# Dealing the first mixer's modulation columns out among the weight units of its second lane

## The chip, the core and the metric

The kernel runs on one core of a Trainium2 chip. The names in the profile are PE (TensorE's matrix multiplications) and PEld (its weight loads), DVE (VectorE), ACT (ScalarE), POOL (GpSimd) and SP (SyncE, which here issues every transfer between the chip's main memory and the core). Each engine works through its own list of instructions in a fixed order; semaphores make one engine wait for another. The metric is the device time of one execution in microseconds (us): the median of the runs, lower is better.

## The reference, cut to what matters

Two layers are computed on a sequence of 1024 positions of width 1024. Each layer is a mixing part and a feed-forward part, and both are steered by six modulation vectors that come from one vector `c`:

```
cond = silu(c)
mod = cond @ w_mod[l] + b_mod[l]
sh1, sc1, gt1, sh2, sc2, gt2 = split(mod, 6)
h = rms_norm(x, norm_g[l, 0]) * (1 + sc1) + sh1
y = mixer_block(h, ...)          # conv, sparse attention, linear attention, gMLP; then @ w_o
x = x + gt1 * rms_norm(y, norm_g[l, 1])
h = rms_norm(x, norm_g[l, 2]) * (1 + sc2) + sh2
y = square(relu(h @ w_up[l])) @ w_down[l]
x = x + gt2 * rms_norm(y, norm_g[l, 3])
```

What matters here are three of the six vectors of layer 0: number 2 (`gt1`), number 3 (`sh2`) and number 4 (`sc2`). They are needed only after the first mixer's output projection `w_o`.

## The kernel before, in words

The sequence is cut into two halves of 512 positions, so that every activation tile is 128 x 512. The order of the work is: first half's mixer of layer 0, `mix(0, 0)`; second half's mixer, `mix(0, 1)`; then feed-forward parts and the mixers of layer 1 in turn. The change lies in `mix(0, 0)` alone.

A projection (`gemm`, L177) takes its weights as two units of 128 x 512. A unit is loaded into a buffer `raw_b` (L158), copied to a rounded high part by ACT (L167), and DVE computes the low part (`sub`, recorded as L131); then twelve matrix multiplications follow, three for each of four slices (L173 to L175). There are two lanes of such weights in `mix(0, 0)`. Lane "a" feeds the sparse attention and `w_o`. Lane "b", with three `raw_b` buffers and four `w_b` buffers, feeds the projections of the linear attention (6), of the gMLP (4) and of the convolution (6): 16 projections, so 32 units. They are independent of the attention, and their multiplications fill PE between the attention's steps.

A modulation vector is eight columns of 128 values. A column (`mod_half`, L242) is two loads of 128 x 512 weights, each reduced on DVE against `cond` (L247) into one number per partition, and one small DVE instruction (L140, `mod<-mp,bmod`) that adds the two numbers and the bias. `mods_now(0, (2, 3, 4), "b")` computes 24 columns behind the convolution with lane "b"'s three `raw_b` buffers: 48 loads and 48 reductions.

After that come, in the program's order: the norm of the attention's output, splitting all eight mixer outputs into high and low parts (`split`, L220), the eight projections by `w_o` in lane "a" (16 units, 192 multiplications, each result copied by ACT at L946 into `yo`), then `between()`, which is the norm and modulation of the second half's input (`rms_R`, L186, and `make_h`, L203), and the residual, which uses vectors 2, 3 and 4.

What stands in which order on an engine is set when the program is built: a scheduler takes instructions whose inputs it believes to be ready by its own model, with earlier code first, and writes one fixed list for each engine. A buffer of a pool goes to the next user when the list says that it is free. All loads stand in one list, that of SP.

Of the kernel before, what the change touches and what calls it, by code (L numbers as in the profile page):

```python
# [35 lines left out]
def trunk_kernel(ctx, tc, xT, c, pos, freq, sel, w_in, conv_w, cmp_pos, cmp_w1, cmp_w2,  # L36
# [10 lines left out]
    def region(name, side="left"):  # L47
        return tc.tile_pool(name=name, bufs=1, reuse_waits="tile", side=side)
# [7 lines left out]
    def ps(tag, shape=(128, 512)):  # L56
        return psum.tile(list(shape), F32, name="ps_" + tag, tag=tag,
                         bufs={"mm": 2, "ff": 2, "s": 2, "t": 1, "pv": 1}[tag])
# [71 lines left out]
    def sub(out, a, b):  # L130
        V.tensor_tensor(out=out, in0=a, in1=b, op=ALU.subtract)  # L131

    def mul(out, a, b, eng=V):
        eng.tensor_tensor(out=out, in0=a, in1=b, op=ALU.mult)
# [4 lines left out]
    def stt(out, a, s, b, op0, op1):  # L139
        V.scalar_tensor_tensor(out=out, in0=a, scalar=s, in1=b, op0=op0, op1=op1)  # L140

    def load(tile, src):
        dma(out=tile, in_=src)
        return tile
# [11 lines left out]
    def wraw(lane, src, shape):  # L156
        raw = lane_pool[lane].tile(shape, F32, name="raw_" + lane, tag="raw_" + lane, bufs=RAWB[lane])
        dma(out=raw, in_=src)  # L158
        return raw

    def wtile(lane, shape):
        return lane_pool[lane].tile(shape, F32R, name="w_" + lane, tag="w_" + lane, bufs=HLB[lane])

    def wunit(lane, src, shape):
        raw = wraw(lane, src, shape)
        hi = wtile(lane, shape)
        A.copy(hi, raw)  # L167
        lo = wtile(lane, shape)
        sub(lo, raw, hi.bitcast(F32))
        return hi, lo  # L170

    def mm3(ps_ap, wh, wl, xh, xl, start, stop):
        PE.matmul(ps_ap, wh, xh, start=start, stop=False)  # L173
        PE.matmul(ps_ap, wh, xl, start=False, stop=False)  # L174
        PE.matmul(ps_ap, wl, xh, start=False, stop=stop)  # L175

    def gemm(ps_ap, lane, src, h, order=(0, 1, 2, 3, 4, 5, 6, 7)):  # L177
        for kh in (order[0] // 4, order[4] // 4):
            hi, lo = wunit(lane, src[:, 4 * kh:4 * kh + 4, :], [128, 4, 128])
            for kk in order:  # L180
                if kk // 4 == kh:
                    k = kk % 4
                    mm3(ps_ap, hi[:, k, :], lo[:, k, :], h[kk][0], h[kk][1],
                        kk == order[0], kk == order[7])

    def rms_R(tiles, inv_n, pt="t", cs=slice(0, T), mk=nt):  # L186
        acc = mk()[:, cs]
        A.activation(acc, tiles[0][:, cs], AF.Square)
        for t in tiles[1:]:
            sq = mk()[:, cs]  # L190
            A.activation(sq, t[:, cs], AF.Square)
            add(acc, acc, sq)
        p = ps(pt)[:, cs]
        with tc.high_priority(offset=400):
            PE.matmul(p, ones, acc, start=True, stop=True)  # L195
            return rstd(p, inv_n, mk()[:, cs])
# [17 lines left out]
    def group_out(y, pt, gain):  # L214
        R = rms_R(y, 1.0 / 256, pt)
        for k in range(2):
            stt(y[k], y[k], gain[:, k:k + 1], R, ALU.mult, ALU.mult)
        return y

    def split(t):  # L220
        hi, lo = htile(), htile()
        A.copy(hi, t)
        sub(lo, t, hi.bitcast(F32))
        return hi, lo
# [17 lines left out]
    def mod_half(l, j, k, mk):  # L242

        mp = work.tile([128, 2], F32, name="mp", tag="mp", bufs=4)
        for kh in range(2):
            raw = mk(w_mod[l, 8 * j + k, :, kh * T:kh * T + T], [128, T])
            V.tensor_tensor_reduce(out=raw, in0=raw, in1=cond[:, kh * T:kh * T + T], scale=1.0, scalar=0.0,  # L247
                                   op0=ALU.mult, op1=ALU.add, accum_out=mp[:, kh:kh + 1])
        stt(par[l]["mod"][:, j, k:k + 1], mp[:, 0:1], mp[:, 1:2], par[l]["bmod"][:, 8 * j + k:8 * j + k + 1],
            ALU.add, ALU.add)  # L250

    def mod_scale(l, j, ks):
        d = par[l]
        m = d["mod"][:, j, ks]
        if j in (1, 4):
            stt(d["A1" if j == 1 else "A2"][:, ks], m, 1.0, d["ng"][:, 0 if j == 1 else 2, ks],
                ALU.add, ALU.mult)
        if j in (2, 5):
            mul(d["G1" if j == 2 else "G2"][:, ks], m, d["ng"][:, 1 if j == 2 else 3, ks])
# [56 lines left out]
        return hs, early  # L316

    def mods_now(l, js, lane):
        for j in js:
            for k in range(8):  # L320
                mod_half(l, j, k, lambda src, shape: wraw(lane, src, shape))
            mod_scale(l, j, slice(0, 8))

    def mods_steps(todo, skip):

# [139 lines left out]
    def gate_part(l, hf, h, gr, rg, lane, early={}):  # L465
        p = early.get(GLA0)
        if p is None:
            p = ps("mm")
            gemm(p, lane, w_in[l, GLA0], h)
        lrT = rg.tile([32, T], F32, name="lrT")  # L470
        V.memset(lrT, 1.0)
        A.copy(lrT[0:16], p[0:16])
        gates = gr.tile([128, 4, 12], F32, name="gates")
        gtmp = gr.tile([128, 4, 12], F32, name="gtmp")
        gs = nt()
        A.copy(gs[0:64], p[0:64])
        gp = ps("t", (128, 4, 64))
        for j in range(4):
            PE.transpose(gp[:, j, :], gs[0:64, 128 * j:128 * j + 128], ident[0:64, 0:64])
        logsig(gates, gp[:, :, 32:44], gtmp)  # L480
        A.activation(gates, gates, AF.Exp)
        return gates, lrT
# [428 lines left out]
    def mix(l, hf, h, between=None, early={}):  # L911
        d = par[l]
        gain = d["gain"]
        with ExitStack() as es:
            gr = es.enter_context(region("gates"))
            if l == 0 and hf == 0:
                sx = ("ff", "ff", "ff")
                with region("wb", "right") as lane_pool["b"]:
                    with region("gl", "right") as rg:
                        gates, lrT = gate_part(l, hf, h, gr, rg, "a", early)  # L920
                        yn = nsa_part(l, hf, h, es.enter_context(region("ns")), gates, early)
                        ol = gla_part(l, hf, h, rg, "b", sx, lrT)
                    with region("cv", "right") as rg, region("gm", "right") as rg2:
                        og = gmlp_part(l, hf, h, rg2, "b", sx)
                        oc = conv_part(l, hf, h, rg, "b", sx)
                    mods_now(0, (2, 3, 4), "b")
            else:
                sx = ("s", "t", "pv")
                with region("cv") as rg, region("gm") as rg2:
                    oc = conv_part(l, hf, h, rg, "a", sx)  # L930
                    og = gmlp_part(l, hf, h, rg2, "a", sx)
                with region("gl") as rg:
                    gates, lrT = gate_part(l, hf, h, gr, rg, "a")
                    ol = gla_part(l, hf, h, rg, "a", sx, lrT)
                yn = nsa_part(l, hf, h, es.enter_context(region("ns")), gates)
            on = group_out(yn, "t", gain[:, 2:4])
            outs = [split(t) for t in oc + og + ol + on]
        res = None
        opening = (l, hf) == (0, 0)
        with region("wo", "right" if opening else "left") as rg:  # L940
            y = []
            for o in range(8):
                p = ps("mm")
                gemm(p, "a", w_o[l, o], outs, (6, 7, 4, 5, 2, 3, 0, 1) if opening else range(8))
                yo = rg.tile([128, T], F32, name="yo", tag="yo", bufs=8)
                A.copy(yo, p)  # L946
                y.append(yo)
            if between is not None:
                res = between()
            with tc.high_priority(offset=-LATER[l, hf]):  # L950
                R = rms_R(y, 1.0 / 1024)
                residual(y, d["G1"], R,
                         lambda k: load(rg.tile([128, T], F32, name="xo", tag="xo", bufs=8 if opening else 4),
                                        (xT[hf] if l == 0 else xb[hf])[:, k, :]), xa[l][hf])
                R = rms_R(y, 1.0 / 1024)
                h2[hf] = make_h(y, R, d["A2"], d["mod"][:, 3, :])
        if opening:
            lane_pool["f"] = pool("ff", side="right")
        return res
# [196 lines left out]
```

## Time and profile before

| What | Value |
|---|---|
| Median of 3 runs | 2634.32 us (2633.39 to 2635.1) |
| The profiled execution's own time | 2634.88 us |
| Its span, first to last instruction | 2633.1 us |
| PE busy over the span | 2488.4 us (95%) |
| DVE busy | 1631.0 us (62%) |
| ACT busy | 1310.5 us (50%) |
| Mean granted clock of TensorE | 0.975 of full speed |

The share of busy time is a mean over stages with different limits; the change is judged from its own stage, the first 360 us. Of the page's 40 slices of 65.8 us the fifth (263 to 329 us) shows PE at 4 tenths and a granted clock of 6 tenths, between slices at 9 and 9. A multiplication's duration in the trace is longer than the distance to the next one, since they overlap; pace is read from the distance between starts.

### The profile page before, as it was taken

How to read it: one execution, taken by the hardware profiler on the slowest of the kernel's cores; microseconds unless marked ns; L12 is line 12 of the kernel's file. 1: busy time of each engine (PE TensorE's matmuls, PEld its weight loads, DVE VectorE, ACT ScalarE, POOL GpSimd, SP SyncE). 2: the span in 40 equal slices, each digit the busy share in tenths (PEclk: the TensorE clock that was granted, in tenths of full speed). 3: DMA queues.
4: the chain of work that ended last, by engine and by line, in shares of the span. 5: the costliest groups of instructions: out<-in, count | busy, mean ns of one | idle time of the engine just before them, and what ended most of it. 6: DMA issues, size and time to landing. Idle time of an engine off the chain costs nothing.

```text
span 2633.1 us, 34406 instructions
## 1 busy us (share of the span) xinstructions
PE 2488.4 (95%) x11834; PEld 1987.3 (75%) x11834; DVE 1631.0 (62%) x3425; ACT 1310.5 (50%) x2657; POOL 53.0 (2%) x65
## 2 busy tenths in 40 slices
PE   5899499999999999999999999999999998899997
PEld 3666277777877878887787878877788876788886
DVE  7676866557888577444676476544567755634445
ACT  3573345445665356344366445444466744443333
POOL 0100000000000000000100000000100000000000
PEclk9899699999999999999999999999999999999999
DMA  8313634345434454322522344322322134433332
GB/s 279 100 46 100 203 117 132 106 140 153 129 123 134 155 164 140 102 85 89 154 83 70 116 152 140 99 84 79 119 77 68 57 108 143 136 97 96 97 97 75
DMA packets 176200, 305.79 MB, mean 116 GB/s; under 512 B 21573, under 2 KB 33434, under 8 KB 176026
## 3 DMA queue, kind: packets, MB, share of 16 engines
q1 hardware_dynamic: 176026, 303.60, 36.7%
q8 instruction: 93, 1.52, 0.2%
q14 instruction: 81, 0.66, 0.1%
HBM read 281.50 MB, written 17.83 MB: 114 GB/s over the span
## 4 chain that ended last, share of the span: by engine, by line
PE 83%; DVE 6%; DMA 4%; issue 1%; ACT 1%; POOL 0%; DVEq 0%; SPq 0%; ACTq 0%; POOLq 0%
PE ps_ff L173 16%; PE ps_ff L174 16%; PE ps_ff L175 16%; PE ps_mm L173 8%; PE ps_mm L175 8%; PE ps_mm L174 8%; DMA raw_f<-in_w_mod_dram 2%; PE ps_pv L783 1%; PE ps_mm L777 1%; PE ps_pv L782 1%; PE ps_s L822 1%; DMA raw_b<-in_w_mod_dram 1%; PE ps_s L824 1%; PE ps_t L777 1%; PE ps_t L195 1%
## 5 line engine op out<-in xcount | busy, mean ns | idle before, releaser
L167 ACT CAST w_f<-raw_f 128x512 fp32r<-128x512 f32 x504 | 311.7, 619 | 426.3 <-PE ps_ff L174 409.2
L131 DVE TENSOR_TENSOR w_f<-raw_f,w_f 128x512 fp32r<-128x512 f32 x504 | 350.4, 696 | 178.7 <-ACT w_f L167 167.9
L173 PE MATMUL ps_ff<-hid,w_f 128*128 128x512 f32 x992 | 395.4, 399 | 21.7 <-DVE yf L137 12.7
L175 PE MATMUL ps_ff<-h,w_f 128*128 128x512 f32 x1024 | 405.4, 396 | 1.2 <-DVE w_f L131 1.2
L173 PE MATMUL ps_ff<-h,w_f 128*128 128x512 f32 x1024 | 403.1, 394 | 0.0
L174 PE MATMUL ps_ff<-h,w_f 128*128 128x512 f32 x1024 | 402.3, 393 | 0.0
L174 PE MATMUL ps_ff<-hid,w_f 128*128 128x512 f32 x992 | 392.4, 396 | 1.5 <-DVE hid L131 1.5
L175 PE MATMUL ps_ff<-hid,w_f 128*128 128x512 f32 x992 | 391.7, 395 | 0.0
L173 PE MATMUL ps_mm<-h,w_a 128*128 128x512 f32 x784 | 318.2, 406 | 32.6 <-ACT yo L946 23.7
L175 PE MATMUL ps_mm<-h,w_a 128*128 128x512 f32 x784 | 317.2, 405 | 6.0 <-DVE w_a L131 6.0
L174 PE MATMUL ps_mm<-h,w_a 128*128 128x512 f32 x784 | 314.8, 403 | 3.6 <-DVE h L131 3.6
L167 ACT CAST w_a<-raw_a 128x512 fp32r<-128x512 f32 x196 | 121.3, 620 | 304.5 <-PE ps_mm L174 278.7
L131 DVE TENSOR_TENSOR w_a<-raw_a,w_a 128x512 fp32r<-128x512 f32 x196 | 135.1, 689 | 179.2 <-ACT w_a L167 173.3
L173 PEld LDWEIGHTS ps_ff<-hid,w_f 128*128 128x128 f32 x992 | 188.1, 190 | 69.8 <-DVE yf L137 15.2
L175 PEld LDWEIGHTS ps_ff<-h,w_f 128*128 128x128 f32 x1024 | 192.3, 188 | 45.5 <-issue 2.9
L173 PEld LDWEIGHTS ps_ff<-h,w_f 128*128 128x128 f32 x1024 | 192.4, 188 | 43.0 <-issue 3.1
L174 PEld LDWEIGHTS ps_ff<-h,w_f 128*128 128x128 f32 x1024 | 192.4, 188 | 42.0 <-issue 2.2
L174 PEld LDWEIGHTS ps_ff<-hid,w_f 128*128 128x128 f32 x992 | 188.3, 190 | 44.6 <-issue 2.9
L175 PEld LDWEIGHTS ps_ff<-hid,w_f 128*128 128x128 f32 x992 | 187.9, 189 | 41.1 <-issue 1.4
L137 DVE TENSOR_TENSOR y<-y,ps_ff 128x512 f32<-128x512 f32 (+1 forms) x208 | 138.0, 664 | 125.0 <-PE ps_ff L175 123.8
L173 PEld LDWEIGHTS ps_mm<-h,w_a 128*128 128x128 f32 x784 | 149.9, 191 | 72.8 <-ACT yo L946 24.1
L175 PEld LDWEIGHTS ps_mm<-h,w_a 128*128 128x128 f32 x784 | 149.8, 191 | 44.5 <-DVE w_a L131 7.7
(390 smaller groups left out, 3610.2 us busy)
## 6 DMA issues: line engine op xcount, KB each, us to landing
raw_f<-in_w_up_dram SPq DMA_DIRECT2D x256, 256.0 KB, 2.7
raw_f<-in_w_down_dram SPq DMA_DIRECT2D x256, 256.0 KB, 2.7
raw_a<-in_w_in_dram SPq DMA_DIRECT2D x132, 256.0 KB, 2.6
raw_f<-in_w_mod_dram SPq DMA_DIRECT2D x112, 256.0 KB, 2.9
raw_a<-in_w_o_dram SPq DMA_DIRECT2D x64, 256.0 KB, 2.7
raw_b<-in_w_mod_dram SPq DMA_DIRECT2D x48, 256.0 KB, 3.1
mw<-in_w_mod_dram SPq DMA_DIRECT2D x16, 512.0 KB, 5.7
bp<-in_cmp_w_dram SPq DMA_DIRECT2D x32, 256.0 KB, 5.7
```

The costliest lines, as they stand in the source:

```text
L131: V.tensor_tensor(out=out, in0=a, in1=b, op=ALU.subtract)
L137: eng.tensor_tensor(out=out, in0=a, in1=b, op=ALU.add)
L167: A.copy(hi, raw)
L173: PE.matmul(ps_ap, wh, xh, start=start, stop=False)
L174: PE.matmul(ps_ap, wh, xl, start=False, stop=False)
L175: PE.matmul(ps_ap, wl, xh, start=False, stop=stop)
L195: PE.matmul(p, ones, acc, start=True, stop=True)
L777: PE.transpose(tp[0:kn, hh, :], cols(h0 + hh), ident)
L782: PE.matmul(pv[:, h0:h0 + nh, :], vst, th[0:kn], start=first[0], stop=False)
L783: PE.matmul(pv[:, h0:h0 + nh, :], vst, tl[0:kn], start=False, stop=last)
L822: PE.matmul(sp[:, 0:w], qh[:, h0 + hh, :], KX[:, 128 * k0:128 * k0 + w], start=True, stop=False)
L824: PE.matmul(sp[:, 0:w], ql[:, h0 + hh, :], KX[:, 128 * k0:128 * k0 + w], start=False, stop=True)
```

## The change

`mods_now` becomes a generator that stops after each column. At every unit of lane "b", after the unit is loaded and split and before its multiplications, `gemm` asks the generator for one column. Vector order becomes 2, 4, 3. Whatever is left after the convolution is then computed as before; with 32 units and 24 columns nothing is left.

```diff
+    beside = {}
+
     def gemm(ps_ap, lane, src, h, order=(0, 1, 2, 3, 4, 5, 6, 7)):
         for kh in (order[0] // 4, order[4] // 4):
             hi, lo = wunit(lane, src[:, 4 * kh:4 * kh + 4, :], [128, 4, 128])
+            if lane in beside:
+                next(beside[lane], None)
...
     def mods_now(l, js, lane):
         for j in js:
             for k in range(8):
                 mod_half(l, j, k, lambda src, shape: wraw(lane, src, shape))
-            mod_scale(l, j, slice(0, 8))
+                if k == 7:
+                    mod_scale(l, j, slice(0, 8))
+                yield
...
                 with region("wb", "right") as lane_pool["b"]:
+                    beside["b"] = mods_now(0, (2, 4, 3), "b")
...
-                    mods_now(0, (2, 3, 4), "b")
+                    for _ in beside.pop("b"):
+                        pass
```

Because the scheduler sets the lists, the diff does not tell where the instructions stand. Line numbers of the changed kernel are a few higher: L251 is what L247 was, L671 what L664 was, L213 what L209 was, L955 what L946 was.

SP's list at the start of lane "b" before (`in_w_in` are a unit's weights, `in_w_mod` those of a column, `p` and `qh`, `ql` belong to the attention):

```order
L158 DMA raw_b<-in_w_in_dram 128x512 x5
L725 DMA p<-in_cmp_pos_dram 64x32
L726 DMA p<-in_cmp_pos_dram 64x31
L725 DMA p<-in_cmp_pos_dram 64x32
L726 DMA p<-in_cmp_pos_dram 64x31
L767 DMA qh<-qh 64x2x128
L767 DMA ql<-ql 64x2x128
```

and of the change (with the numbers that tell tiles of one name apart):

```order
L158 DMA raw_b_1552<-in_w_in_dram 128x512
L158 DMA raw_b_1559<-in_w_mod_dram 128x512
L158 DMA raw_b_1562<-in_w_mod_dram 128x512
L158 DMA raw_b_1578<-in_w_in_dram 128x512
L158 DMA raw_b_1585<-in_w_mod_dram 128x512
L158 DMA raw_b_1588<-in_w_mod_dram 128x512
L158 DMA raw_b_1607<-in_w_in_dram 128x512
L158 DMA raw_b_1614<-in_w_mod_dram 128x512
L158 DMA raw_b_1617<-in_w_mod_dram 128x512
L732 DMA p_786<-in_cmp_pos_dram 64x32
L733 DMA p_786<-in_cmp_pos_dram 64x31
```

Ahead of the attention's first four loads stood five loads in three buffers; now there are nine in the same three buffers. The pattern of one unit and two column loads goes on for 24 units.

DVE's list at the same place before (`gates`, `qr`, `qh`, `ql`, `VS`, `VW` belong to the attention):

```order
L131 TENSOR_TENSOR KW<-p,KW 64x512
L131 TENSOR_TENSOR w_b<-raw_b,w_b 128x512 x2
L140 SCALAR_TENSOR_TENSOR gates<-ps_t,gtmp 128x48
L137 TENSOR_TENSOR qr<-p 128x512
L140 SCALAR_TENSOR_TENSOR g<-ps_ff,g 128x512
L664 STREAM_SHUFFLE p<-qs 128x512
L131 TENSOR_TENSOR VS<-ps_t,VS 128x4x64
```

and of the change, with numbers:

```order
L131 TENSOR_TENSOR w_b_1556<-raw_b_1552,w_b_1554 128x512
L251 ISA raw_b_1559,mp_1558<-raw_b_1559,cond_130 128x512
L251 ISA mp_1558 128x1
L251 ISA raw_b_1562,mp_1558<-raw_b_1562,cond_130 128x512
...
L140 SCALAR_TENSOR_TENSOR gates_662<-ps_t_666,gtmp_663 128x48
L137 TENSOR_TENSOR qr_717<-p_719,p_720 128x512
L140 SCALAR_TENSOR_TENSOR g_1534<-ps_ff_1529,g_1535 128x512
L140 SCALAR_TENSOR_TENSOR mod0_100<-mp_1558,bmod0_97 128x1
L671 STREAM_SHUFFLE p_726<-qs_716 128x512
L131 TENSOR_TENSOR w_b_1582<-raw_b_1578,w_b_1580 128x512
L251 ISA raw_b_1585,mp_1584<-raw_b_1585,cond_130 128x512
```

A column's two reductions now stand among the attention's own DVE work, and each reads a load that was queued behind an earlier buffer's release.

ACT's list at the output projection before (`h<-nt` is `make_h` of the second half, `yo` the copy that frees a result buffer of PE; the last of the eight `h` rows and the two behind it):

```order
L199 ACTIVATE nt_3083<-ps_t_3081,eps_78 128x512
L200 ACTIVATE nt_3083<-nt_3083 128x512
L167 CAST w_a_2845<-raw_a_2843 128x512
L209 ACTIVATE h_3088<-nt_3086,mod0_100 128x512
...
L209 ACTIVATE h_3130<-nt_3128,mod0_100 128x512
L946 COPY yo_2783<-ps_mm_2746 128x512
L946 COPY yo_2822<-ps_mm_2785 128x512
```

and of the change:

```order
L955 COPY yo_2783<-ps_mm_2746 128x512
L203 ACTIVATE nt_3083<-ps_t_3081,eps_78 128x512
L204 ACTIVATE nt_3083<-nt_3083 128x512
L213 ACTIVATE h_3088<-nt_3086,mod0_100 128x512
L167 CAST w_a_2827<-raw_a_2825 128x512
L213 ACTIVATE h_3094<-nt_3092,mod0_100 128x512
L167 CAST w_a_2845<-raw_a_2843 128x512
L213 ACTIVATE h_3100<-nt_3098,mod0_100 128x512
L955 COPY yo_2822<-ps_mm_2785 128x512
```

All eight `h` activations stood ahead of the first two copies of results; now the first copy stands ahead of all of them and the second behind three. DVE's list there has the same work without the 48 reductions, and SP's list goes straight on with the loads of `w_o`. From `mix(0, 1)` on the lists of both kernels soon are the same.

## Rows read from the trace of the kernel before

**Rows 1.** Busy time by stage: length, PE, PEld, DVE, ACT, POOL, clock, DMA

```profile
core 0: us, PE busy (x) PEld busy (x) DVE busy (x) ACT busy (x) POOL busy (x), PEclk, DMA share, GB/s
75.00:103.00 28.00, 17.50 (x192) 15.31 (x192) 19.70 (x59) 13.59 (x47) 7.26 (x6) 0.68 0.29 78
103.00:145.00 42.00, 42.00 (x219) 34.08 (x222) 27.74 (x87) 29.52 (x80) 0.00 (x0) 0.97 0.25 69
145.00:180.00 35.00, 34.99 (x226) 26.08 (x218) 29.40 (x94) 26.90 (x71) 2.90 (x5) 1.00 0.14 46
...
200.00:236.00 36.00, 35.02 (x180) 27.01 (x180) 23.03 (x37) 17.08 (x32) 0.00 (x0) 0.98 0.20 65
236.00:256.20 20.20, 20.14 (x89) 16.34 (x87) 12.34 (x28) 4.86 (x8) 0.00 (x0) 1.00 0.41 132
256.20:319.30 63.10, 19.59 (x55) 12.29 (x55) 56.77 (x152) 23.17 (x39) 0.64 (x1) 0.63 0.64 202
```

**Rows 2.** PE's timeline, 255 to 356: start, duration, idle before

```profile
255.76 0.39 PE L175 MATMUL ps_mm<-h,w_b 128*128 128x512 f32 x1
261.00 2.07 PE L195 MATMUL ps_ff<-nt,ones 128*128 128x512 f32 x2 [4.85 <-DVE nt L137]
...
276.54 0.79 PE L173 MATMUL ps_mm<-h,w_a 128*128 128x512 f32 x1 [7.02 <-ACT h L222]
280.92 0.80 PE L174 MATMUL ps_mm<-h,w_a 128*128 128x512 f32 x1 [3.58 <-DVE h L131]
...
295.20 0.40 PE L175 MATMUL ps_mm<-h,w_a 128*128 128x512 f32 x1
319.29 0.80 PE L173 MATMUL ps_mm<-h,w_a 128*128 128x512 f32 x1 [23.70 <-ACT yo L946]
...
324.42 0.39 PE L173 MATMUL ps_mm<-h,w_a 128*128 128x512 f32 x1
...
354.99 0.40 PE L175 MATMUL ps_mm<-h,w_a 128*128 128x512 f32 x1
```

**Rows 3.** ACT's timeline, 256 to 322: start, duration, idle before

```profile
258.40 0.63 ACT L191 ACTIVATE nt<-of 128x512 f32<-128x512 f32 x1 [7.26 <-DVE of L134]
...
318.04 0.72 ACT L209 ACTIVATE h<-nt,mod 128x512 fp32r<-128x512 f32 x1 [0.68 <-DVE nt L140]
318.67 1.05 ACT L946 COPY yo<-ps_mm 128x512 f32<-128x512 f32 x2
```

**Rows 4.** DVE's groups, 246 to 320: busy, mean ns, idle before

```profile
L247 DVE CUSTOM_DVE_ANT_0 raw_b<-raw_b,cond 128x512 f32<-128x512 f32 x48 | 32.9, 687 | 6.8 <-DMA raw_b<-in_w_mod_dram 6.7
...
L140 DVE SCALAR_TENSOR_TENSOR mod<-mp,bmod 128x1 f32<-128x1 f32 x23 | 5.4, 233 | 0.0
...
L247 DVE DVE_READ_ACCUMULATOR2_ANT mp<- 128x1 f32 x48 | 3.9, 82 | 0.0
```

**Rows 5.** DVE's timeline, two steps of the attention's norm and split

```profile
275.10 1.41 DVE L140 SCALAR_TENSOR_TENSOR qs<-qs,gain,nt 128x512 f32<-128x512 f32 x2
...
280.18 0.68 DVE L131 TENSOR_TENSOR h<-qs,h 128x512 fp32r<-128x512 f32 x1
```

**Rows 6.** What PE waited for, 75 to 103: total, times, longest

```profile
PE ps_t L683 <- DVE gates L140: 4.8, 1, 4.8
PE ps_mm L710 <- DMA p<-in_cmp_pos_dram: 3.4, 1, 3.4
```

**Rows 7.** SP's timeline, 72 to 90

```profile
73.82 10.08 SPq L158 DMA_DIRECT2D raw_b<-in_w_in_dram  x5
88.08 0.58 SPq L725 DMA_DIRECT2D p<-in_cmp_pos_dram  x1
```

**Rows 8.** ACT's casts of weight units (L167), 103 to 180: length, busy, count

```profile
103.00:180.00 77.00, 9.82 (x16) 0.98 0.20 58
```

**Rows 9.** Tile `raw_b`, 60 to 245: from issue to landing, and DVE's low parts

```profile
L131 DVE TENSOR_TENSOR w_b<-raw_b,w_b x29: 659/689/1751, 81.2 to 243.1; 128x512 fp32r<-128x512 f32 x29
...
DMA to landing us min/median/max: 2.4/2.6/3.5
```

## The prediction, made before the changed kernel ran

> **What bounds the kernel now.** I read the busy time by stage first, because the page's 95% for PE is a mean. From 103 to 180 us PE is busy for all of 77 us (42.00 and 34.99) while DVE has 57.1 of them (27.74 + 29.40); from 200 to 236 it is much the same, 35.02 of 36 against 23.03 [rows 1]. From 256.2 to 319.3 it is turned round: DVE is busy for 56.8 of 63.1 us, PE for 19.6, at a granted clock of 0.63 [rows 1]. So there are two stages: one in which PE is full and DVE has room, and behind it one in which DVE is full and PE waits.
>
> PE's timeline shows what the second stage costs. The last multiplication of lane "b" starts at 255.76. The first by `w_o` starts at 276.54 and waits once more, until 280.92; after 24 per result for two results PE stops at 295.2 (start) and waits 23.7 us until 319.29 for `yo`; the last of the 192 starts at 354.99 [rows 2]. ACT's timeline tells why `yo` is late: the copy is behind `h` activations, the last of which waited for DVE [rows 3]. And DVE's groups tell why it is late: in 246 to 320 us, 48 reductions of 687 ns each and 6.7 us of waiting for their loads [rows 4].
>
> **What the change takes away.** All 48 reductions leave the second stage. I work out when the last `w_o` multiplication would start, with the end of lane "b" at its old place, 256.2.
>
> - *The way to `w_o`.* Before, 280.92 - 256.2 = 24.7 us. Without reductions between, the steps in a row are: the convolution's product on DVE 0.7, one Square on ACT 0.6 [rows 3], one addition on DVE 0.7, the sum over partitions on PE 2.1 [rows 2]: 4.1 us. The same norm of the attention's output, which takes its buffers from the first one: two Squares 1.2, addition 0.7, sum 2.1: 4.0. The two activations of the root and three others that stand between them in ACT's list: 5 x 0.63 = 3.1. The two gains 1.4, three splits ahead of the attention's and then its own, 4 x 0.68 = 2.7 [rows 5]. Sum 15.3; I take 16 with hand-overs. Saved: 24.7 - 16 = 8.7 us.
> - *The wait for `yo`.* In the changed list the first copy stands ahead of all `h` activations and the second behind three. The `h` work on DVE is 16 instructions of about 0.75 us and a few low parts of weights, while PE needs 24 x 0.233 = 5.6 us for each result (pace: 131 steps from 324.42 to 354.99 [rows 2]). I leave 1.5 us of the 23.7 standing. Saved: 22.2.
> - *One slow start.* After 319.29 twelve multiplications took 5.13 us until 324.42, where twelve at the later pace take 2.80 [rows 2]. That is 0.43 against 0.233 us for each, the lower of the clock's two levels (1.2 GHz) against the higher (2.4 GHz), right behind PE's idle time. The first stretch, from 280.92, begins behind idle time too. One of the two slow starts goes: 2.3.
>
> Together 33.2 us. What is late next there is DVE's `h` work. Bounds: 25 if a third of the wait for `yo` stays, 38 if the way to `w_o` shrinks to 12 us.
>
> **What it adds elsewhere.** Each column costs DVE two reductions and the small instruction, 2 x 0.687 + 0.233 = 1.61 us (reading the accumulator, 82 ns, overlaps [rows 4]); 24 columns 38.6 us. No row shows columns beside the attention, so I bound it. From below: nothing, if they fall in DVE's idle time, which is 8.3 + 14.3 + 5.6 + 13.0 = 41 us in the four stages to 236 [rows 1], or even a little less than nothing, since the list of PE is a new one; I give that 2 us. From above: all 38.6 on the path, since the attention's own steps go through DVE in order. To choose, I ask how full DVE gets at all in this trace: 56.77 of 63.1 us, 90%, in the stage in which it was the limit [rows 1]. Taken stage by stage:
>
> - 75 to 103 us: three columns. PE waits here for `gates` (4.8 us) and for `p` (3.4 us) [rows 6]. `gates` now has two reductions ahead of it and one low part fewer: 2 x 0.69 - 0.69 = 0.7. SP's list has nine loads ahead of `p` instead of five; five ended in time for `p` at 88.08 [rows 7]. The third unit's loads need buffers that DVE releases, one more round of landing 2.6 [rows 9] and reduction. I take 3 us for the stage, up to 6.
> - 103 to 180: 16 units are cast here [rows 8]. I count 15 columns (three went before): 15 x 1.61 = 24.2, and 57.1 + 24.2 = 81.3 us of DVE work in 77 us. At 90% that takes 90 us: 13 longer.
> - 200 to 236: six columns, 23.0 + 9.7 = 32.7, at 90% 36.3 for 36: nothing.
>
> Sum 16 us. That stands beside 0 and 38.6; the price is nearer to the middle because in 103 to 180 the work doesn't fit, and elsewhere it does. The three `raw_b` buffers have a price of their own, below under the slower side.
>
> By the Trainium skill, "Perfetto Trace Analysis", section "Identifying the Most-Contended Engine", a busy PE row says little and the busy share of weight loads more. That share is (34.08 + 26.08) / 77 = 78% [rows 1]; read that way PE has a fifth of its time in reserve and a delay of 16 us would be made good. The stretch from 236 to 256.2 decides against it: 16.34 of 20.2, 81%, while multiplications follow each other without a gap [rows 1]. So about 80% is this kernel's full PE, and nothing is made good. If the rule held, the time would be that of the better case below.
>
> **Sum.** 2634.9 (the profiled execution; the median of the runs is 2634.3) - 33.2 + 16.3 = 2618.0 us. From 400 us on the lists are the same, so nothing further changes.
>
> **Rivals.**
>
> *All of it fits (better).* The columns fill DVE's idle 41 us and only the first stage loses 3. For it: they nearly fit in sum. Against: 81.3 us of work in 77. 2634.9 - 33.2 + 3 = 2605.
>
> *The tail keeps a wait.* `h` on DVE and the weights of `w_o` take the place of the reductions and hold `yo` for another 12 us. For it: DVE still has the 16 `h` instructions and four low parts of weights, some 15 us, while PE needs 5.6 for a result. Against: the copies are spread over the list. 2634.9 - 21 + 16 = 2630, within the bound of no change.
>
> *The three buffers starve lane "b" (slower).* Before, all three held weights. Now a unit and its two loads share them, and PE's list has the units' multiplications between the attention's. The place is the stretch of the first 24 units, from 77 to about 230 us: 6.4 us each. A round of one buffer is landing 2.6 to 3.5 us [rows 9], 0.33 of issue, a reduction 0.69, or for a unit a cast 0.62 and a low part 0.69: 4.3 to 5.1 with nothing queued. That is below 6.4 and costs nothing. But where both loads of a column go through one buffer one after the other, a round is 2 x (3.0 + 0.33 + 0.69) = 8.0: 24 x (8.0 - 6.4) = 38 us longer, and 2634.9 - 33.2 + 38 = 2640. The gain is eaten from 24 p - 154 = 33, so from 7.8 us for each unit. Against it: it would have to happen at nearly every unit, and the scheduler hands a buffer to whichever load its list has next, so a column's two loads mostly get two buffers. The Trainium skill, "Perfetto Trace Analysis", section "Optimization Strategy", says that the same gap coming back on the engine that should be full can mean too few buffers; that is this case, and the trace of before, with weights alone in the buffers, shows no such gap in 103 to 180.
>
> *The change doesn't do what it says.* 24 columns need 24 units and there are 32; the lists show them spread. Below 1 in 100.
>
> **Chances.** The forecast with a loss of 6 to 26 us: 0.60 (2607 to 2628). All fits: 0.17. The tail keeps a wait, or both costs are high: 0.13, of which 0.08 is within 0.2% (5.3 us, about what a measurement of this kernel can tell from no change). Starved lane: 0.10, of which 0.08 is slower by more than that and 0.02 within. That makes faster 0.82, within 0.10, slower 0.08. The range that leaves 0.2 out goes from 2603 to 2632.
>
> **What the changed profile would show.** Right: no stretch with a PE idle of over 5 us between the convolution's last multiplication and `w_o`'s last but the one ahead of `w_o`, some 13 to 16 us long; no reductions behind the convolution; `yo` not waited for by more than 2 us; DVE at 90% or more in what was 103 to 180, and that stage longer by 8 to 18 us, PE waiting in it in many short pieces for DVE (`sm`, `bp`, `w_a`, `w_b`). Wrong: the convolution's end later by over 30 us, with ACT waiting for `raw_b` loads at L167 and SP for DVE (starved lane); or the end of lane "b" at its old place (all fits); or a long wait at `yo` (tail). The steps that I hold least sure are the 90% and the 1.5 us.

## The result and the profile after

The changed kernel takes 2615.96 us (median of 4 runs, 2614.26 to 2618.0) against 2634.71 (4 runs, 2633.39 to 2637.07) in the same job: the ratio is 0.9929, 95% interval 0.9916 to 0.9941, so 0.7% faster. The profiled execution has a span of 2616.3 us against 2633.1.

Two distances of PE say where that comes from. Lane "b"'s last multiplication starts at 275.16 us instead of 255.76: 19.4 later. The last of the 192 by `w_o` starts at 337.26 instead of 354.99: 17.7 earlier. So 37.1 us were saved behind lane "b" and 19.4 lost ahead of it.

PE's timeline of the changed kernel, with all waits of over 0.5 us from 220 to 346 us (start, duration, line, tiles, in brackets the idle time and who ended it), answers to [rows 2]:

```profile
221.56 0.50 PE L790 MATMUL ps_pv<-w_a,VS 128*128 128x512 f32 x1 [2.00 <-DVE w_a L131]
223.17 0.80 PE L789 MATMUL ps_pv<-w_a,VS 128*128 128x512 f32 x1 [0.68 <-ACT w_a L786]
...
275.16 0.39 PE L177 MATMUL ps_mm<-h,w_b 128*128 128x512 f32 x1
277.71 1.12 PE L199 MATMUL ps_ff<-nt,ones 128*128 128x512 f32 x2 [2.17 <-DVE nt L137]
281.47 2.05 PE L199 MATMUL ps_t<-nt,ones 128*128 128x512 f32 x2 [2.63 <-DVE nt L137]
288.61 0.79 PE L175 MATMUL ps_mm<-h,w_a 128*128 128x512 f32 x1 [5.09 <-ACT h L226]
290.56 0.79 PE L176 MATMUL ps_mm<-h,w_a 128*128 128x512 f32 x1 [1.16 <-DVE h L131]
...
337.26 0.40 PE L177 MATMUL ps_mm<-h,w_a 128*128 128x512 f32 x1
```

From 290.56 on PE does not wait any more, where before it stood 23.7 us for `yo` [rows 2]. ACT's timeline shows why: the first copy stands ahead of all `h` activations, and the next ones behind two or three, none of which waits long [rows 3]:

```profile
298.09 0.58 ACT L955 COPY yo<-ps_mm 128x512 f32<-128x512 f32 x1
...
300.83 0.72 ACT L213 ACTIVATE h<-nt,mod 128x512 fp32r<-128x512 f32 x1 [0.82 <-DVE nt L140]
...
305.15 0.56 ACT L955 COPY yo<-ps_mm 128x512 f32<-128x512 f32 x1
...
310.14 0.58 ACT L955 COPY yo<-ps_mm 128x512 f32<-128x512 f32 x1
```

The stages of the changed kernel (stretch, its length, busy time of PE, weight loads, DVE, ACT, POOL, then granted clock, DMA share and GB/s) answer to [rows 1]:

```profile
75.00:107.80 32.80, 16.74 (x190) 14.35 (x189) 25.24 (x73) 13.30 (x44) 8.31 (x6) 0.67 0.40 116
107.80:190.00 82.20, 77.89 (x440) 59.31 (x439) 71.22 (x240) 50.43 (x137) 3.49 (x6) 0.99 0.49 150
190.00:220.00 30.00, 23.48 (x105) 16.17 (x104) 21.76 (x63) 20.71 (x51) 1.93 (x2) 0.89 0.22 67
220.00:255.00 35.00, 32.55 (x157) 24.90 (x157) 25.42 (x54) 13.27 (x25) 0.00 (x0) 0.90 0.36 106
```

Once lane "b" has begun, PE nowhere stands long, but from 145 us on it stands in many short pieces, and in the stretches from 190 the granted clock is 0.89 and 0.90. The two longest of these waits between 170 and 220 us are:

```profile
204.56 0.50 PE L789 MATMUL ps_pv<-w_a,VC 32*128 32x512 f32 x1 [2.42 <-ACT w_a L786]
...
209.01 1.11 PE L784 MATMUL ps_t<-ident,bp 128*128 128x128 f32 x4 [1.75 <-DVE z L407]
```

The chain of waits tells more than the busy time. It goes back from the last instruction to what released it. Here is the summary of its part from 107.8 to 275.4 us in the changed kernel:

```profile
by line: DMA raw_b<-in_w_mod_dram 16.3%; PE ps_mm L175 9.6%; PE ps_mm L177 9.4%; PE ps_mm L176 9.3%; DVE raw_b L251 9.0%; DVE w_b L131 4.8%; DVE w_a L131 4.1%; DVE bp L836 3.8%; issue 3.2%; PE ps_t L784 2.5%; DVE g L134 2.1%; DVE g L596 1.8
```

and a few of its pieces in order of time (start, duration, what):

```profile
112.91 2.62 DMA raw_b<-in_w_mod_dram
...
115.56 0.69 DVE raw_b L251
...
116.29 2.81 DMA raw_b<-in_w_mod_dram
...
119.12 0.69 DVE raw_b L251
...
134.29 3.79 DMA raw_b<-in_w_mod_dram
...
138.10 0.69 DVE raw_b L251
```

In these pieces a column's load lands in 2.6 to 3.8 us (the longest piece of the whole part, at 145.44, has 5.16), DVE reduces it in 0.69, that frees the buffer for the next load, and so on. Landing takes 16.3% of 167.6 us, 27 us, and the reductions 9.0%, 15 us. Before, PE's own multiplications made up most of this part.

### The profile page after: what moved, and what is told of

It is laid out like the page before. It is cut to its first block, busy times and chain, and to the rows that moved or that the text cites. A ratio compares the mean times of both kernels' runs of the same rounds, so it can differ in the third digit from the quotient of the medians.

```text
span 2616.3 us, 34392 instructions
## 1 busy us (share of the span) xinstructions
PE 2488.0 (95%) x11834; PEld 1985.6 (76%) x11834; DVE 1631.3 (62%) x3425; ACT 1308.9 (50%) x2657; POOL 53.9 (2%) x65
## 4 chain that ended last, share of the span: by engine, by line
PE 83%; DVE 8%; DMA 5%; ACT 2%; issue 1%; SPq 0%; DVEq 0%; ACTq 0%
PE ps_ff L175 17%; PE ps_ff L176 17%; PE ps_ff L177 17%; PE ps_mm L176 7%; PE ps_mm L177 7%; PE ps_mm L175 7%; DMA raw_f<-in_w_mod_dram 2%; PE ps_mm L784 1%; DMA raw_b<-in_w_mod_dram 1%; PE ps_pv L790 1%; PE ps_pv L789 1%; PE ps_s L829 1%; PE ps_t L199 1%; PE ps_s L831 1%; PE ps_t L784 1%
## 5 line engine op out<-in xcount | busy, mean ns | idle before, releaser
L167 ACT CAST w_f<-raw_f 128x512 fp32r<-128x512 f32 x504 | 311.8, 619 | 430.5 <-PE ps_ff L176 409.0
L167 ACT CAST w_a<-raw_a 128x512 fp32r<-128x512 f32 x196 | 121.3, 620 | 297.7 <-PE ps_mm L176 276.8
L131 DVE TENSOR_TENSOR w_a<-raw_a,w_a 128x512 fp32r<-128x512 f32 x196 | 135.0, 690 | 171.2 <-ACT w_a L167 167.3
```

## The experiments

Times of different jobs are compared by their ratio to the kernel before in the same job. The rest of the program behind `w_o` took between 2271.5 and 2280.5 us in profiles with the columns in the first mixer (span less the start of the last `w_o` multiplication), a scatter that follows none of the edits; so effects are read from PE's timeline. One table for all, in us but for the ratio: "First" and "Last" are the starts of lane "b"'s first and last multiplication, "Lane" is the distance between them, and "Last of `w_o`" is the start of the last of the 192 by `w_o`.

| Kernel | First | Last | Lane | Last of `w_o` | Ratio, 95% interval |
|---|---|---|---|---|---|
| before | 102.57 | 255.76 | 153.2 | 354.99 | 1 |
| changed | 107.82 | 275.16 | 167.3 | 337.26 | 0.9929 [0.9916, 0.9941] |
| no columns | 102.81 | 255.88 | 153.1 | 318.75 | 0.9862 [0.9847, 0.9877] |
| no loads | 125.56 | 279.45 | 153.9 | 342.38 | 0.9953 [0.9938, 0.9968] |
| lane a's buffers | 114.84 | 275.38 | 160.5 | 338.25 | 0.9943 [0.9928, 0.9958] |
| from the 4th unit | 104.12 | 274.03 | 169.9 | 336.92 | 0.9929 [0.9913, 0.9946] |
| from the 9th unit | 103.91 | 276.30 | 172.4 | 338.42 | 0.9934 [0.9915, 0.9952] |
| 8 of 512 products | 103.24 | 266.94 | 163.7 | 328.88 | 0.9884 [0.9869, 0.9899] |
| 256 of 512 | 106.00 | 273.15 | 167.2 | 336.26 | 0.9907 [0.9893, 0.9922] |
| loads alone | 103.39 | 270.50 | 167.1 | 333.39 | 0.9918 [0.9901, 0.9935] |
| four buffers | 108.00 | 272.87 | 164.9 | 335.92 | 0.9923 [0.9908, 0.9937] |
| POOL and ACT | 108.19 | 282.18 | 174.0 | 345.29 | 0.9962 [0.9948, 0.9976] |
| next mixer, 2 buffers | 102.80 | 255.81 | 153.0 | 324.49 | 1.0015 [1.0005, 1.0024] |
| next mixer, 1 buffer | 104.53 | 256.87 | 152.3 | 325.82 | 1.0055 [1.0040, 1.0070] |

**What there is to gain.** The columns left out: in `mods_now`

```diff
-                mod_half(l, j, k, lambda src, shape: wraw(lane, src, shape))
+                V.tensor_copy(par[l]["mod"][:, j, k:k + 1], par[l]["bmod"][:, 8 * j + k:8 * j + k + 1])
```

> This kernel leaves out the 24 columns of modulation vectors 2, 3 and 4 of layer 0: each is set to its bias by one copy of 128 x 1 on DVE, at the same places in the code as in the change. It measures what the columns cost the first lane stage in all, and what the tail gains when nothing of them is there. Theory (the tail gains 37 us, the columns cost the lane stage 19): the lane's last multiplication starts within 3 us of its old place, 255.8, and the last by w_o near 318, so the time is 2635 - 37 = 2598 us, 2593 to 2602. Rival (the 19 us are not the columns' work or loads but the new order of the lists, which moves other things too): the lane still ends after 262 and the time is 2605 or more.

Measured 2594.41 us (2591.93 to 2597.95). Lane "b" stands where it did before the change to 0.3 us, and the tail behind it is that of the changed kernel, only 19.3 us earlier at its start and 18.5 at its end:

```profile
255.88 0.39 PE L177 MATMUL ps_mm<-h,w_b 128*128 128x512 f32 x1
258.43 1.19 PE L199 MATMUL ps_ff<-nt,ones 128*128 128x512 f32 x2 [2.17 <-DVE nt L137]
262.25 2.04 PE L199 MATMUL ps_t<-nt,ones 128*128 128x512 f32 x2 [2.63 <-DVE nt L137]
269.38 0.79 PE L175 MATMUL ps_mm<-h,w_a 128*128 128x512 f32 x1 [5.09 <-ACT h L226]
271.34 0.79 PE L176 MATMUL ps_mm<-h,w_a 128*128 128x512 f32 x1 [1.16 <-DVE h L131]
```

So the tail and the lane are two separate terms, and the whole lateness of the lane is the columns'.

**DVE's time or the loads, first try.** Reductions without loads (they read `cond` alone), then loads into lane "a"'s three idle buffers:

```diff
+    def mod_dry(l, j, k):
...
+            raw = work.tile([128, T], F32, name="raw_a", tag="raw_a", bufs=3)
+            V.tensor_tensor_reduce(out=raw, in0=cond[:, T - kh * T:2 * T - kh * T], in1=cond[:, kh * T:kh * T + T],
...
-                mod_half(l, j, k, lambda src, shape: wraw(lane, src, shape))
+                mod_dry(l, j, k)
```

> The 48 reductions of the 24 columns stay on DVE at the same places in the code, with the same size, but read cond, which is resident, instead of loaded weights; their 48 loads are left out (so vectors 2, 3 and 4 of layer 0 are other numbers), and they write into raw_a buffers that stand idle there, so lane b's three buffers hold weights alone. Theory A (DVE is full: the 19 us are the 38 us of added DVE work that does not fit beside the attention): nothing is gained by leaving out the loads, 2613 to 2619 us. Theory B (DVE has room for the work; the 19 us are its waits for loads that were issued late because a unit and a column share three buffers, 18 us by the trace): 2598 to 2604 us, with DVE as busy as in the change and no wait for loads.

```diff
-                    beside["b"] = mods_now(0, (2, 4, 3), "b")
+                    beside["b"] = mods_now(0, (2, 4, 3), "a")
```

> The change, with one edit: the columns are loaded into lane a's three raw_a buffers, which hold next to nothing in this stage, and lane b's raw_b buffers hold weights alone. Work, loads and their number are those of the change. Theory A (DVE is full): 2613 to 2619 us. Theory B (shared buffers): most of the 18.2 us in which DVE waited for the columns' loads and of the 11.0 us for casts goes, 2599 to 2606 us; the lane's last multiplication starts before 265 instead of 275.2. A third possibility (SP's one list holds up the loads, whichever buffers they have): 2610 to 2616 us with SP waiting as long as before.

Measured 2618.56 (2617.16 to 2620.37) and 2616.74 (2613.04 to 2617.86). Both times are theory A's, but the profile shows that neither run put the question. Without a load or a unit's buffer to wait for, the scheduler took the reductions as early as it could. In the first run DVE's instructions on these tiles (stretch, length, busy time) are:

```profile
50.00:75.00 25.00, 8.20 (x13) 1.00 0.41 136
75.00:107.80 32.80, 17.32 (x24) 0.75 0.34 114
107.80:125.60 17.80, 3.28 (x5) 0.60 0.33 76
```

With those ahead of 50 us (the remaining ones of the 48), all stand ahead of lane "b", which begins 22.8 us later than without columns and then takes its 153.9 us. In the second, the lane begins 12.0 us later and loses 7.5 on its way. What these two do show: the reductions cost at that place too, and a lane whose buffers and whose way are free of columns loses under 1 us.

**Where the columns stand.** Empty steps of the generator, three and then eight:

```diff
     def mods_now(l, js, lane):
+        for _ in range(3):
+            yield
```

> The change, with the first column asked for by the fourth unit instead of the first (three empty steps ahead), so that no column's load or reduction stands ahead of the attention's first loads and norms; all 24 columns still fit in 32 units. If the 5.2 us by which the lane's first multiplication came later (107.8 after 102.6) are due to the first three columns, it starts near 103 again and the time falls by about 5, to 2609 to 2613 us. If the columns are as dear wherever they stand (theory A, and theory B too where the later units are packed closer), the time stays within 3 us of 2616.

> The first column comes with the ninth of the 32 units instead of the first, so that the last eight fall beside the projections of the gMLP and the convolution, where DVE has 13 to 14 of 35 us free. Theory A1 (a column costs only where DVE is nearly full): 2600 to 2606. Theory A2 (about half of a column's DVE time ends on the path wherever it stands ahead of the attention's end): 16 of 24 columns still stand there, 2606 to 2612. Theory B: 2610 to 2616.

Measured 2612.43 (2611.53 to 2613.45) and 2620.25 (2612.41 to 2621.42). The first time looks like the one expected, but PE's timeline says otherwise: 3.7 us come back at the lane's start, 2.6 are lost on its way, and `w_o` ends only 0.3 earlier than in the changed kernel; the ratio is the same. With eight, the lane takes longer still (172.4). Up to the start of its eleventh projection, where fewer columns stand beside the attention, it has lost less than the changed kernel: 9.1 us against 13.3, both against the kernel without columns. Of the other 10.2, 9.0 are lost behind the start of its fourteenth projection, at the convolution, where DVE is busy for only 17.5 of 25.1 us (251.2 to 276.3), and with that theory A1 falls. Four of PE's five waits from 250 to 276 us of that kernel (6.1 us together) show a new price:

```profile
255.03 0.51 PE L175 MATMUL ps_mm<-h,w_b 128*128 128x512 f32 x1 [0.98 <-ACT w_b L167]
259.19 0.50 PE L175 MATMUL ps_mm<-h,w_b 128*128 128x512 f32 x1 [0.84 <-ACT w_b L167]
265.19 0.50 PE L175 MATMUL ps_mm<-h,w_b 128*128 128x512 f32 x1 [2.70 <-ACT w_b L167]
269.26 0.50 PE L175 MATMUL ps_mm<-h,w_b 128*128 128x512 f32 x1 [0.75 <-ACT w_b L167]
```

At the convolution PE has nothing but lane "b" to do. A unit takes it 2.7 us there (5.4 for a projection in the kernel before), and three loads per unit through three buffers don't come that fast: from 245 to 276 us ACT waits 13.9 us in five places for the units' own weights.

**The size of the reductions.** Loads, buffers and places stay; the sums take 8, then 256 of 512 products:

```diff
-            V.tensor_tensor_reduce(out=raw, in0=raw, in1=cond[:, kh * T:kh * T + T], scale=1.0, scalar=0.0,
+            V.tensor_tensor_reduce(out=raw[:, 0:8], in0=raw[:, 0:8], in1=cond[:, kh * T:kh * T + 8], scale=1.0, scalar=0.0,
```

> Leaves out of each column's two sums all but the first 8 of 512 products; the 48 loads, their buffers and their place stay. With the columns left out altogether 2594.4 us were measured, the changed kernel stands at about 2616. Theory A (what costs is the time that a reduction takes on DVE): 48 x (0.745 - some 0.15) = 29 of 36 us of DVE work go, so 2594 to 2601, lane b's last multiplication at 256 to 262. Theory B (what costs is that the loads share lane b's three buffers, and DVE and ACT wait for them in order): nothing changes, 2612 to 2618, lane b's end at 272 to 276.

> Leaves out the second half of the products of each of the two sums: reductions of 128 x 256, about 0.4 us instead of 0.745, while loads, buffers and places stay. Theory A in proportion: about half of lane b's lateness of 19.4 us, so 2603 to 2609. If DVE has to be full before anything costs, half the work (71 + 12 less of 82 us between 108 and 190) costs nearly nothing: 2595 to 2601. Theory B: 2612 to 2618.

Measured 2606.54 (2602.1 to 2606.83) and 2611.89 (2609.89 to 2612.85): the first between the theories, the second at the lower edge of theory B. The lane's end is 11.1, 17.3 and 19.3 us later than without columns for reductions of 8, 256 and 512. DVE's group of reductions in the run with 8 (busy time, mean ns | idle time before):

```profile
L251 DVE CUSTOM_DVE_ANT_0 raw_b<-raw_b,cond 128x8 f32<-128x8 f32 x48 | 9.7, 205 | 28.6 <-DMA raw_b<-in_w_mod_dram 28.3
```

and of the changed kernel, to set beside [rows 4]:

```profile
L251 DVE CUSTOM_DVE_ANT_0 raw_b<-raw_b,cond 128x512 f32<-128x512 f32 x48 | 35.6, 745 | 18.4 <-DMA raw_b<-in_w_mod_dram 18.2
```

A quarter of the work (9.7 of 35.6 us) leaves over half of the lateness (11.1 of 19.3), because the time that DVE no longer works it mostly stands at the next load: 28.3 instead of 18.2 us. And the price splits by place. The later start of the lane (5.0 us) goes with DVE's work: 0.4 us with 8 products, 3.2 with 256. The loss on the way (14.3) hardly does: 10.6 and 14.1.

These losses do not stand at the same place, though. Against the kernel without columns, the lane of the changed kernel is 1.1 us ahead at the start of its eighth projection and 13.3 behind at that of its eleventh; with 8 products it is 8.1 behind at the eighth already, and 10.5 at the eleventh. The lists are new ones in each kernel, so it is not shown that the 10.6 us are a part of the same 14.3.

**Loads alone, and a fourth buffer.** The sums left out and each load read by a small POOL instruction, so that DVE never stands at one; then a fourth `raw_b` with everything computed:

```diff
+            if beside:
+                mul(raw[:, 0:32], raw[:, 0:32], cond[:, 0:32], eng=P)
...
+        if beside:
+            V.tensor_copy(par[l]["mod"][:, j, k:k + 1], bm)
```

> Leaves the columns' sums out but keeps their 48 loads in lane b's three buffers: each is read by one small POOL instruction, and DVE only copies the bias, so that DVE never waits for a column's load. Without loads and sums lane b ended at 255.9 us, with loads and 8-element sums at 266.9. Theory C1 (the loads cost because DVE waits for them in its list): the end at 255 to 259, ratio 0.986 to 0.9875. Theory C2 (they cost because they take buffers and landing time from the units' weights): 264 to 268, ratio 0.988 to 0.990.

```diff
-    RAWB = {"a": 3, "f": 5, "b": 3}
+    RAWB = {"a": 3, "f": 5, "b": 4}
...
-        mp = work.tile([128, 2], F32, name="mp", tag="mp", bufs=4)
+        mp = work.tile([128, 2], F32, name="mp", tag="mp", bufs=2)
```

> Lane b gets a fourth raw_b buffer (and mp two instead of four, which makes the room). With reductions of 8 elements lane b still ended 11.1 us later than without columns, so I split the lateness of 19.3 us in two. Theory C (half or more of it comes from the loads in the three buffers: DVE stands at a column's load in its fixed list): loads are issued a round earlier, DVE's wait for column loads falls from 18.2 us to under 9, lane b's last multiplication from 275.2 to 264 to 271, ratio 0.988 to 0.991. Theory A (DVE's time alone): the end stays at 273 to 277, ratio 0.992 to 0.994.

Measured 2610.01 (2607.69 to 2611.52) and 2612.6 (2607.47 to 2614.18). Loads alone keep 14.6 of the 19.3 us, more than theory C2 expected, but part of it is the experiment's own. POOL's list is as fixed as DVE's, and the linear attention's `g` is cleared behind reads that wait. POOL's timeline of this run:

```profile
166.34 0.25 POOL L134 TENSOR_TENSOR raw_b<-raw_b,cond 128x32 f32<-128x32 f32 x1 [3.38 <-issue]
169.46 0.25 POOL L134 TENSOR_TENSOR raw_b<-raw_b,cond 128x32 f32<-128x32 f32 x1 [2.87 <-DMA raw_b<-in_w_mod_dram]
169.65 1.45 POOL L597 MEMSET g<- 128x512 f32 x3
```

and the wait that PE has for it:

```profile
172.02 1.19 PE L605 MATMUL ps_ff<-g 128*128 128x512 f32 x1 [5.10 <-DVE g L601]
```

Without those 5.1 us and the 1.8 by which PE's waits for POOL's `g` grew (3.0 against 1.2), some 7 of 14 us on the lane's way remain for loads that no DVE instruction waits for; that remainder is an estimate. The fourth buffer takes DVE's wait for column loads from 18.2 to 12.5 us and 2.5 us off the lane's way: less than theory C asked for, and the ratio can't be told from the changed kernel's. What the two `mp` buffers fewer cost in that run was not tried by itself.

**Another engine, another mixer.** The product on POOL and its sum on ACT:

```diff
+                mul(raw, raw, cond[:, kh * T:kh * T + T], eng=P)
+                A.activation(raw, raw, AF.Identity, accum_out=mp[:, kh:kh + 1])
```

> A column's product goes to POOL (about 1.7 us for 128 x 512, as POOL's two products of the attention take) and its sum to ACT (about 0.62 us, as its other 128 x 512 instructions); DVE keeps only the small addition. Everything is computed. Theory A: DVE is as free as with no columns, ACT gets 30 us more where it had some 45% free: 2596 to 2606, lane b's end at 256 to 266. Theory B: the buffers are held longer (POOL and ACT in a row instead of one DVE instruction), so 2616 to 2630. If instead ACT's work costs as DVE's did, 2608 to 2612.

Measured 2625.57 (2622.61 to 2628.57), lane "b" 26.3 us late: freeing DVE made it worse. ACT's group of these sums:

```profile
L253 ACT ACTIVATE raw_b<-raw_b 128x512 f32<-128x512 f32 x48 | 30.2, 629 | 23.6 <-POOL raw_b L134 23.5
```

Now ACT stands 23.5 us in its list, for POOL, which took 1382 ns for a product and waited itself for the loads. Theory A can't explain that.

Last, the columns moved in the code to the second mixer, among lane "a"'s units, with buffers of their own, and the first half's residual behind the second mixer's gMLP:

```diff
...
+            def mrow(src, shape):
+                t = rg.tile(shape, F32, name="raw_m", tag="raw_m", bufs=2)
+                dma(out=t, in_=src)
+                return t
+            beside["a"] = mods_now(0, (2, 4, 3), mrow)
+            pending.append(tail)
...
```

> All computed. The columns leave the first mixer: they are dealt out among lane a's units of the second mixer, with two buffers of their own, and the first half's residual, which needs them, follows the second mixer's gMLP. There PE is full from 400 to 550 us while DVE is busy for 84 of 150. If a column costs only where PE waits for DVE in a row of dependent steps: as without columns, ratio 0.985 to 0.988. If it costs half its DVE time wherever it stands: ratio 0.991 to 0.994.

> As the run before with one buffer instead of two, so that a reduction comes only every 4 us or so and DVE has half as much of it at a time. If two reductions to a unit are already hidden: the same as with two buffers to 0.1%. If the first units of the second mixer starve with two: faster than with two by 0.1 to 0.4%.

Measured 2634.87 (2632.46 to 2639.55) and 2646.97 (2643.65 to 2648.78): both misses. The scheduler again took the reductions earlier than the code has them: with two buffers they run from 258.2 to 353.7 us, 32 of the 48 ahead of the second mixer's first unit at 324.72, and with one from 259.3 to 426.2, only 8 of them behind 400. So neither run put the columns beside the PE that was full from 400 to 550 us. With two buffers `w_o` ends 12.8 us earlier than in the changed kernel, and between 400 and 500 us more than that is lost. Its stages there:

```profile
400.00:450.00 50.00, 36.97 (x136) 26.87 (x135) 36.26 (x57) 27.03 (x49) 0.00 (x0) 0.90 0.28 95
450.00:500.00 50.00, 44.44 (x248) 35.52 (x249) 29.17 (x63) 27.69 (x52) 2.25 (x4) 0.90 0.39 123
```

In the changed kernel PE was busy for all 100 us. None of these columns' reductions is left from 400 on. Beside the splitting of weights, DVE's and ACT's largest groups there are the residual's and those of the norm and modulation behind it, and PE's longest wait, 8.3 us, is for an `nt` of the linear attention's gates, which uses the same three buffers and ACT. That points to the residual's move and not to the columns, but the columns without that move weren't tried. No complete kernel here is shown to beat the changed one.

## Why the prediction came out

The time (2618.0 forecast, 2615.96 measured, span 2616.3) is right, and so are the signs of both terms. The reason given for the larger half of the cost is not.

- *The way to `w_o`.* From 275.6 to 290.56 it took 15.0 us where I took 16; saved 9.7, forecast 8.7. The waits on it, 2.2, 2.6, 5.1 and 1.2 us, are the ones that the steps counted in a row left to PE.
- *The wait for `yo`.* 0 instead of 1.5; saved 23.7, forecast 22.2. `h` was late nowhere, since the copies are spread over the list.
- *The slow start.* From 290.56 to 337.26 took 46.7 us; before, 74.07 less the wait is 50.4. Saved 3.7, forecast 2.3: the first starts are 0.43 apart until 294.12 only, nine instead of fourteen, and the second slow start is gone. Together 37.1 against 33.2, within the bound of 38.
- *75 to 103 us.* 5.2 us against 3. The loads ahead of `p` cost 2.7 and `gates` 0.6 more wait, as worked out. Not foreseen was a third place: `p` (L134) stands behind a reduction in DVE's list, which waits 2.05 us for its load at 104.51, and PE waits 3.46 for that `p`; another wait fell by 1.3 [rows 6]. That these 5 us are DVE's is shown by two runs that keep the 48 loads but take DVE's work away: with 8 products the lane starts 0.4 us later than without columns, and with loads alone 0.6.
- *103 to 180 us.* This is the step that failed: "at 90% that takes 90 us: 13 longer". The lane's way did get 14.2 us longer, but not here and not for that reason. Lane "b"'s eighth projection starts 62.5 us after its first, before 63.7: nothing is lost up to 170. DVE was busy for 71.2 of 82.2 us from 107.8 to 190, 87%, where 90% was named as the sign. All of it is lost between the starts of the eighth and the eleventh, from 170 to 238, where I had put nothing. These two starts on PE's timeline, before:

```profile
166.24 0.49 PE L173 MATMUL ps_mm<-h,w_b 128*128 128x512 f32 x1
...
220.06 0.48 PE L173 MATMUL ps_mm<-h,w_b 128*128 128x512 f32 x1
```

  and in the changed kernel:

```profile
170.27 0.50 PE L175 MATMUL ps_mm<-h,w_b 128*128 128x512 f32 x1 [0.90 <-DVE g L134]
...
238.53 0.49 PE L175 MATMUL ps_mm<-h,w_b 128*128 128x512 f32 x1
```

  What fell behind earlier was the attention. The first of each of its four pairs of copies on ACT's timeline:

```profile
130.08 0.37 ACT L901 COPY qs<-ps_pv 64x256 f32<-64x256 f32 x1 [0.76 <-PE ps_pv L790]
...
167.61 0.35 ACT L901 COPY qs<-ps_pv 64x256 f32<-64x256 f32 x1
...
206.26 0.37 ACT L901 COPY qs<-ps_pv 64x256 f32<-64x256 f32 x1
...
256.77 0.37 ACT L901 COPY qs<-ps_pv 64x256 f32<-64x256 f32 x1 [0.46 <-PE ps_pv L790]
```

  They are 7.7, 13.1, 15.1 and 23.3 us later than before (122.40, 154.52, 191.15, 233.46). While units of lane "b" were at hand, PE filled the time with them; from 180 to 225 us it waited for `w_a`, `z` and `g` (2.42 us at 204.56, 1.75 at 209.01, 2.00 at 221.56), and behind such a wait its starts were 0.43 us apart instead of 0.23 (210.35 to 211.63), the lower clock level.
- *Why the attention fell behind.* With reductions of 8 products the way still loses 10.6 us where it lost 14.3, though at another place, and on the chain of waits of that run column loads still have the largest share of any transfer:

```profile
by line: PE ps_mm L175 14.8%; PE ps_mm L176 14.0%; PE ps_mm L177 13.8%; DMA raw_b<-in_w_mod_dram 12.8%; PE ps_t L784 4.4%; PE ps_pv L789 3.3%; PE ps_pv L790 2.8%; DVE w_b L131 2.7%; PE ps_ff L612 2.1%; issue 2.0%; PE ps_ff L199 1.7%; PE ps_
```

  So the chains and the totals point mostly to the loads' landing, which stands in fixed lists: an engine that has come to a column waits for its load (28.3 us of DVE's time in that run), whatever else is ready. Moving the wait to POOL and ACT did not take the loss away. How much of it is this standing, and how much that the units' own weights come later through the shared buffers, the runs don't settle: in the run that was to tell them apart POOL's list cost some of the difference. By the difference of the totals DVE's own work is the other 4 us on the way; that is an estimate, since the two losses stand at different places.
- *The rivals.* "All fits" had the lane's end at its old place plus 3 us; it came 19.4 later. "The tail keeps a wait" has nothing for it. "The three buffers starve lane b" had the round right (2.6 to 3.8 us landing, 0.69 reduction, which the chain shows one behind the other) and its price for the whole lane wrong, 14 us for all causes together and not 38; I set it aside because weights alone showed no gap. At the convolution, with columns from the ninth unit, it happened as described: units of 2.7 us against three loads. By the Trainium skill, "Perfetto Trace Analysis", section "Optimization Strategy", such a gap coming back can mean too few buffers. That is so in these rows; beside the attention, where PE has other work, the gaps don't show on PE and have to be read from the chain.

Both terms were too small by about 3 us and 4 us, and they cancel: that the time fits to 2 us is partly luck.

## What to carry to other kernels

Work dealt out among other work brings its loads along: price a dealt-out step also by its landing time in a fixed list and by the buffers that it shares, and look for both in the chain of waits. An engine's free share doesn't say whether work fits beside a chain of dependent steps; here a quarter of the work had over half of the cost. And an experiment that takes a wait away also frees the scheduler to put the work elsewhere: read where it stands before reading the time.

## What was not expected of the hardware

Two of the 48 reductions took 1.75 us instead of 0.69, and both ran beside a product on POOL. (Two more, at 170.13 and 179.02, took 0.86 and 1.17, beside another instruction of POOL.) DVE's timeline of the changed kernel, 82 to 90 us:

```profile
82.48 1.75 DVE L251 CUSTOM_DVE_ANT_0 raw_b<-raw_b,cond 128x512 f32<-128x512 f32 x1
...
88.26 1.75 DVE L251 CUSTOM_DVE_ANT_0 raw_b<-raw_b,cond 128x512 f32<-128x512 f32 x1
```

and POOL's:

```profile
81.98 1.70 POOL L134 TENSOR_TENSOR p<-qs,cs 128x512 f32<-128x512 f32 x1 [0.69 <-DVE KW L131]
...
87.84 1.62 POOL L134 TENSOR_TENSOR p<-p,cs 128x512 f32<-128x512 f32 x1 [0.74 <-DVE p L671]
```

The first stands ahead of `gates` and makes it 1.06 us later; PE's wait for `gates` grew by 0.6. How much of that reaches the lane's start is not shown: with 8 products the same reduction took 1.23 us instead of 0.17, and the lane started only 0.4 later than without columns. The Trainium skill, "SBUF — State Buffer", section "SBUF: two separate sides", says that a DVE instruction with two SBUF inputs and a GpSimd instruction that reads SBUF take turns, each for its whole length; these rows agree: the first reduction ends 0.55 us behind POOL's product, and so does the second. With columns from the ninth unit, when these products are over, no reduction took more than 0.69 us.

The reductions' time falls less than their size: medians of 692, 424 and 166 ns for 512, 256 and 8 elements, with 82 to 83 ns each for reading the accumulator.
